# mLSTM output gate and spatial u projection with channels as rows, and the spatial mix with swapped operands

## The chip, the cores and the metric

The kernel runs as one program on one core of a Trainium2 chip. Times are device microseconds (us) of that core, from several executions of the same program; one more execution is recorded by the hardware profiler and gives the trace. Engines are named as in the trace: PE (TensorE, matrix products) with PEld (its weight loads), DVE (VectorE), ACT (ScalarE), POOL (GpSimd) and SP (SyncE, which here issues nearly all DMAs).

## The reference, cut to what matters

Two layers act on 512 latent tokens (x) and, in layer 0 only, on 256 context tokens as well (in layer 1 the context is still read, but has no output). Each layer makes one wide projection of the normalised input (1024 columns in), feeds four mixers, gates each of their outputs, projects and sums. Two of the mixers matter here:

```
# B: spatial gating, chunks of 128 tokens, 4 groups of 128 channels
u = gelu(u)
v = layer_norm(gelu(v), ln_g, ln_b)
mixed = einsum('gts,bnsgc->bntgc', w_s, v in chunks) + b_s.T[:, :, None]
yg = u * mixed

# D: mLSTM, 4 heads of 128 channels
hn = rms_norm(h_forward + h_backward, m_norm per head)
ym = sigmoid(m_o) * hn
```

u, v and m_o are 512 columns each of the wide projection. Everything is float32.

## The kernel before, in words

**Projections.** A product of two float32 matrices is made of three PE products of rounded float32 parts (high by high, high by low, low by high), so a tile of output over the 1024 inputs (8 blocks of 128) costs 24 matmuls. There are two ways to write it. `tok_mm` (line 411) keeps a block of 128 tokens stationary and streams 256 columns of weights: the result has tokens as rows. `x_seg` and `seg_mm` (lines 440 and 424) keep 128 columns of weights stationary and stream the tokens, 512 of x (`SEGX`) or 256 of context (`SEGC`): the result has channels as rows. Weights come in units of 256 columns; `take` and `emit_load` load a unit ahead in two halves, which ACT (line 224) and DVE (line 225) split into parts.

**The parts that change.** `mo_unit` (line 573) projects m_o with tokens as rows: per unit and per token tile 24 matmuls of 256 columns, a tanh on ACT (line 581), a product with the norm's weights on DVE (line 582), and a DMA to DRAM in 512-byte rows (line 583). There are 2 units of 6 token tiles in layer 0 and 2 of 4 in layer 1. `mlstm_scan` reads these rows back per head (line 1019), multiplies them into the normalised state with one DVE instruction per chunk (line 1060), turns each chunk with a PE transpose (line 1066), copies the result out of PSUM with ACT (line 1067) and writes it to `ydram[3]`.

`spatial` (line 619) projects v with tokens as rows, normalises it (`spatial_norm`), and mixes the tokens of a chunk with `spatial_mix` (line 692): four plain float32 products with the mixing weights stationary and v streamed, and four ACT instructions of 128 columns that add the bias, one number per row (line 699). Then it projects u with tokens as rows (line 654), applies gelu (`gelu2`, line 610, on tiles of 256 columns: lines 613 to 617), multiplies by the mixed v (line 662), and `turn_out` (line 673) turns the product with two PE transposes (line 676), halves it on ACT out of PSUM (line 678) and writes it to `ydram[2]` (line 679). That is 20 tiles in all, 12 in layer 0 and 8 in layer 1. `turn_out` lags two tiles behind, in the list `tails`.

**Buffers.** Tiles come from pools of fixed numbers of buffers: `T1` (256 columns, 7 buffers), `ST` (512 columns, 3 buffers, shared by the gate, early and m units, the rotary stage and the norm), `M` (768 columns, 8 buffers), `BIG` (4 buffers), and in PSUM `DB` (3 banks) for projections.

**Order.** The program is written as two interleaved threads: the mixers (attention, then the mLSTM scans) and the dense units in the order of `FILL_ORDER` (line 71), in proportion to costs given by hand (`TOK_US`, `seg_us`, `RATIO`). The mixers' instructions get a higher priority, and the tile framework then draws up the order of each engine's instructions from an estimated timeline (`schedule_with_timeline_sim=True`, line 1557). In layer 1 the spatial units run among the dense units, beside the window attention. In layer 0 they run inside `merge` (line 1266), at the places that `AFTER` (line 70) gives: branches are merged in the order 0, 1, 3, 2 with 8 steps j each, v after steps 6 and 7 of the first, `g_u0` after step 0 and `g_u1` after step 3 of the third. The last two tails are run after steps 4 and 5 (line 1343). The fourth branch is the spatial one: it reads `ydram[2]` back (line 1279) with its gate (line 1280), multiplies (line 1287) and splits into parts (lines 1288 and 1289).

Of the kernel before, what the change touches and what calls it, by code (L numbers as in the profile page):

```python
# [19 lines left out]
XT = 4  # L20
NT = 6
# [62 lines left out]
def tile_hybrid_block(ctx, tc, A, out):  # L84
# [61 lines left out]
    # constants  # L146
# [131 lines left out]
    def side(units):  # L278
        """Units of later uses, their rows of weights summed up by VectorE, in small steps."""
# [144 lines left out]
    def seg_mm(wh, wl, mh, ml, nk, seg):  # L424
        """One column tile over one token segment."""
# [44 lines left out]
    def rotate(ear, nh, t, g, tabs, copies):  # L470
        """Second stage: norm, rotary and the split into copies of high and low parts."""
# [30 lines left out]
    def drain(n2, n3):  # L502
        """Runs the waiting stages of earlier tiles, all but the last n2 and n3."""
# [106 lines left out]
    def gelu2(dst, ps, acc=None):  # L610
        """dst = 2 gelu(ps), and its sum over the columns"""
        e, sq = T1(), T1()
# [6 lines left out]
    def spatial(l, ydram, nq, tails, res):  # L619
# [18 lines left out]
        vsum = const.tile([128, NT, 2], F32, tag="vsum", name="vsum")  # L638
        for i in range(2):
            w = in_unit(l, f"g_v{i}")  # L640
            for t in range(nq):
                ps = tok_mm(w, 256, t)
                idle_drain()
                gelu2(V[:, t, i * 256:(i + 1) * 256], ps[:, :256], vsum[:, t, i:i + 1])
                if i == 1:
                    spatial_norm(V[:, t, :], vsum[:, t, :], lng, lnb)
                    if t >= 2:
                        spatial_mix(V[:, t - 2, :], sgw, sgb)
                yield TOK_US + (0.9 if i else 0.0)
            yield  # L650
        for i in range(2):
            w = in_unit(l, f"g_u{i}")
            for t in range(nq):
                ps = tok_mm(w, 256, t)
                if i == 0 and t < 2:
                    spatial_mix(V[:, nq - 2 + t, :], sgw, sgb)
                if len(tails) > 1:
                    tails.pop(0)()
                gu = T1()
                gelu2(gu, ps[:, :256])  # L660
                v = V[:, t, i * 256:(i + 1) * 256]
                dve.tensor_mul(v, v, gu)
                dst = ydram[2, 2 * i:2 * i + 2, :, t * 128:(t + 1) * 128]
                tails.append(lambda v=v, dst=dst: turn_out(v, dst))
                yield TOK_US + 0.22
            if i == 1 and res is not None:
                while tails:
                    tails.pop(0)()
# [4 lines left out]
    def turn_out(v, dst):  # L673
        pt = DB()
        for g in range(2):
# [885 lines left out]
```

## Time and profile before

| | us |
|---|---|
| three executions | 2069.32, 2072.67, 2073.26 |
| their median | 2072.67 |
| span of the profiled execution | 2072.0 |
| PE busy in it | 2006.9 |
| DVE busy | 1321.5 |
| ACT busy | 978.5 |

The span runs from the first to the last instruction of the profiled execution. A busy time is the union of an engine's instructions. A matmul's record is longer than the distance to the next one, since they are pipelined: what a matmul costs is read from the distance between starts. Layer 0 lasts to about 1235 us: the first 60 us are the prologue, then come the interleaved threads to about 860, the merge to about 1160 and the output projection. Layer 1 repeats this, without a prologue.

### The profile page before, as it was taken

What the parts mean: (1) busy time and instruction counts of PE and PEld (TensorE: products, weight loads), DVE (VectorE), ACT (ScalarE), POOL (GpSimd) and SP (SyncE); (2) the same over time, 40 slices, a digit from 0 to 9 for tenths busy, and PEclk for the clock granted to TensorE, in tenths of its full rate; (3) what the DMA queues carried; (4) which work ended last, traced back from release to release, by engine and by line L of the source; (5) the groups of instructions that cost most, each with busy time, mean ns of one, the idle gap of its engine ahead of it and who ended that gap; (6) DMA issues with size and microseconds to landing.
All of it is one profiled execution on the core that took longest, in us unless ns stands there. A gap on an engine that the chain in (4) does not pass through costs nothing. (4 is left out here: it accounts for less than half of the span.)

```text
span 2072.0 us, 34558 instructions
## 1 busy us (share of the span) xinstructions
PE 2006.9 (97%) x13196; PEld 1816.9 (88%) x13196; DVE 1321.5 (64%) x2861; ACT 978.5 (47%) x2195; POOL 69.0 (3%) x76
## 2 busy tenths in 40 slices
PE   7999999999999999999999999999999999999998
PEld 4998998999999898889998999989989898887777
DVE  5766766676556665648545588667676575555765
ACT  6565554344444444324432376655554465433333
POOL 0200100000000000001000022000000000000000
PEclk9999999999999999999999999999999999999999
DMA  7212223323333534665334352223334325447745
GB/s 279 73 44 85 81 86 115 123 98 112 122 117 96 172 122 149 198 206 184 114 116 140 123 190 67 86 96 112 92 121 139 123 90 161 147 147 224 246 136 178
DMA packets 133142, 274.97 MB, mean 133 GB/s; under 512 B 16176, under 2 KB 52208, under 8 KB 132592
## 3 DMA queue, kind: packets, MB, share of 16 engines
q1 hardware_dynamic: 132688, 272.69, 40.5%
q8 instruction: 104, 1.70, 0.3%
q14 instruction: 62, 0.51, 0.1%
q10 hardware_dynamic: 288, 0.07, 0.0%
HBM read 219.33 MB, written 53.37 MB: 132 GB/s over the span
## 5 line engine op out<-in xcount | busy, mean ns | idle before, releaser
L238 PE MATMUL d<-xh,wh 128*128 128x512 f32 (+1 forms) x1504 | 538.0, 358 | 0.1
L238 PE MATMUL d<-xh,wl 128*128 128x512 f32 (+1 forms) x1504 | 535.9, 356 | 0.0
L238 PE MATMUL d<-xl,wh 128*128 128x512 f32 (+1 forms) x1504 | 535.2, 356 | 0.0
L225 DVE TENSOR_TENSOR wl<-wr,wh 128x1024 fp32r<-128x1024 f32 (+3 forms) x274 | 294.5, 1096 | 67.9 <-ACT wh L224 64.8
L224 ACT CAST wh<-wr 128x1024 fp32r<-128x1024 f32 (+3 forms) x274 | 248.8, 950 | 182.5 <-PE s L238 81.7
L238 PEld LDWEIGHTS d<-xh,wh 128*128 128x128 f32 x1504 | 285.6, 190 | 35.0 <-DVE st L604 0.3
L238 PEld LDWEIGHTS d<-xh,wl 128*128 128x128 f32 x1504 | 285.4, 190 | 34.4
L238 PEld LDWEIGHTS d<-xl,wh 128*128 128x128 f32 x1504 | 285.6, 190 | 33.7
L238 PE MATMUL d<-wh,xh 128*128 128x256 f32 (+1 forms) x992 | 287.1, 290 | 5.6 <-ACT t L614 1.4
L238 PE MATMUL d<-wl,xh 128*128 128x256 f32 (+1 forms) x992 | 283.3, 286 | 0.3 <-DVE wl L225 0.3
L238 PE MATMUL d<-wh,xl 128*128 128x256 f32 (+1 forms) x992 | 282.5, 286 | 0.6 <-DVE xl L401 0.4
L238 PEld LDWEIGHTS d<-wh,xh 128*128 128x128 f32 x992 | 189.8, 192 | 7.2 <-ACT t L614 1.6
L238 PE MATMUL s<-big,wh 128*128 128x512 f32 x720 | 184.1, 362 | 9.6 <-DVE big L1289 8.0
L238 PEld LDWEIGHTS d<-wh,xl 128*128 128x128 f32 x992 | 190.0, 192 | 1.3 <-DVE xl L401 0.8
L238 PEld LDWEIGHTS d<-wl,xh 128*128 128x128 f32 x992 | 190.3, 192 | 0.9 <-DVE wl L225 0.5
L780 DVE TENSOR_TENSOR m<-s,m 128x768 fp32r<-128x768 f32 (+2 forms) x144 | 119.4, 836 | 95.2 <-ACT m L779 94.6
L744 ACT ACTIVATE m<-s,yx 128x768 f32<-128x768 f32 (+3 forms) x160 | 120.2, 752 | 92.8 <-DVE yx L742 46.0
L238 PEld LDWEIGHTS s<-big,wh 128*128 128x128 f32 x720 | 120.4, 191 | 32.8 <-DVE big L1289 9.2
L738 DVE TENSOR_REDUCE yx<-s 128x1 f32<-128x768 f32 (+3 forms) x160 | 122.5, 765 | 34.9 <-PE s L238 33.8
L779 ACT CAST m<-s 128x768 fp32r<-128x768 f32 (+2 forms) x144 | 100.8, 704 | 88.6 <-PE s L776 88.0
L238 PE MATMUL b<-m,v 128*128 128x256 f32 (+1 forms) x768 | 132.3, 286 | 4.0 <-ACT m L779 4.0
L238 PE MATMUL s<-big 128*128 128x256 f32 (+2 forms) x680 | 119.7, 304 | 1.3 <-ACT big L496 0.7
(289 smaller groups left out, 3035.0 us busy)
## 6 DMA issues: line engine op xcount, KB each, us to landing
wr<-in_w_in_dram SPq DMA_DIRECT2D x100, 512.0 KB, 4.2
wr<-in_w_mg_dram SPq DMA_DIRECT2D x50, 512.0 KB, 4.3
wr<-in_w_mod_dram SPq DMA_DIRECT2D x42, 512.0 KB, 5.3
wr<-in_w_out_dram SPq DMA_DIRECT2D x32, 512.0 KB, 3.7
th<-st SPq DMA_DIRECT2D x50, 256.0 KB, 4.7
wr<-in_w_bp_dram SPq DMA_DIRECT2D x50, 256.0 KB, 3.9
wr<-in_w_br_dram SPq DMA_DIRECT2D x28, 384.0 KB, 4.2
m<-th SPq DMA_DIRECT2D x26, 384.0 KB, 6.0
```

What stands on the lines that cost most here:

```text
L224: act.copy(wh[:, sl], raw[:, :hn])
L225: dve.tensor_sub(wl[:, sl], raw[:, :hn], rd(wh[:, sl]))
L238: pe.matmul(o, l, r, start=start, stop=stop)
L738: dve.reduce_max(out=mx, in_=ps[:, :n], axis=AX.X)
L744: act.activation(P, ps[:, :n], AF.Exp, bias=nm[:, 0:1], scale=sc, accum_out=sm)
L779: act.copy(ph, pt[:, :n])
L780: dve.tensor_sub(pl, pt[:, :n], rd(ph))
```

## The change

`mo_unit` and the u part of `spatial` use `x_seg`: channels as rows, weights stationary, tokens streamed in 512 or 256 columns. The norm's weights become one number per row, loaded once per layer by a DMA of single elements. The mLSTM output is normalised, transposed and then multiplied by its gate straight out of PSUM. `spatial_mix` swaps its operands (v stationary, mixing weights streamed), so its result has channels as rows like u; its bias now lies along the columns, so `bias_rows` makes a tile with the halved bias spread over rows (four DVE instructions, one float32 product, one ACT copy, once per layer), and one DVE instruction of 512 columns halves and adds. `turn_out`, `tails` and the transposes of line 676 are gone. In layer 0, where `V` has no tile to spare, the bias tile is a buffer of the `M` pool. The new tiles of `mo_unit` and of the u part (two per segment) come from `ST` in place of `T1`. The diff also drops comments and docstrings, and so moves line numbers; that part is left out here.

```diff
-    def mo_unit(l, i, omd, nq):
+    def mo_unit(l, i, omd, segs):
         w = in_unit(l, f"m_o{i}")
-        g = T1()
-        sy.dma_start(out=g, in_=bc(A["m_norm"][l, :, i * 256:i * 256 + 256], [128, 256]))
-        for t in range(nq):
-            ps = tok_mm(w, 256, t)
-            idle_drain()
-            th = T1()
-            act.activation(th, ps[:, :256], AF.Tanh, scale=0.5)
-            dve.scalar_tensor_tensor(out=th, in0=th, scalar=1.0, in1=g, op0=ALU.add, op1=ALU.mult)
-            sy.dma_start(out=omd[2 * i:2 * i + 2, :, t * 128:(t + 1) * 128].rearrange("h p d -> p h d"), in_=v3(th, 2))
-            yield TOK_US
+        if i == 0:
+            g = const.tile([128, 4], F32, tag="mnorm", name="mnorm")
+            sy.dma_start(out=g, in_=A["m_norm"][l].rearrange("o (h e) -> e (o h)", h=4))
+            res_g[l] = g
+        g = res_g[l]
+        for c in range(2):
+            h = 2 * i + c
+            for seg in segs:
+                ps = x_seg(w, c, seg)
+                idle_drain()
+                n = seg.stop - seg.start
+                th = ST()[:, :n]
+                act.activation(th, ps, AF.Tanh, scale=0.5)
+                dve.tensor_scalar(th, th, 1.0, g[:, h:h + 1], op0=ALU.add, op1=ALU.mult)
+                sy.dma_start(out=omd[h][:, seg], in_=th)
+                yield seg_us(seg)
...
+        sgr = V[:, nq, :] if nq < NT else M(512)
...
                 if i == 1:
                     spatial_norm(V[:, t, :], vsum[:, t, :], lng, lnb)
+                    if t == 1:
+                        bias_rows(sgb, sgr)
                     if t >= 2:
-                        spatial_mix(V[:, t - 2, :], sgw, sgb)
+                        spatial_mix(V[:, t - 2, :], sgw, sgr)
...
             w = in_unit(l, f"g_u{i}")
-            for t in range(nq):
-                ps = tok_mm(w, 256, t)
-                if i == 0 and t < 2:
-                    spatial_mix(V[:, nq - 2 + t, :], sgw, sgb)
-                if len(tails) > 1:
-                    tails.pop(0)()
-                gu = T1()
-                gelu2(gu, ps[:, :256])
-                v = V[:, t, i * 256:(i + 1) * 256]
-                dve.tensor_mul(v, v, gu)
-                dst = ydram[2, 2 * i:2 * i + 2, :, t * 128:(t + 1) * 128]
-                tails.append(lambda v=v, dst=dst: turn_out(v, dst))
-                yield TOK_US + 0.22
+            for c in range(2):
+                g = 2 * i + c
+                for seg in segs:
+                    ps = x_seg(w, c, seg)
+                    if g == 0 and seg.start == 0:
+                        for t in range(nq - 2, nq):
+                            spatial_mix(V[:, t, :], sgw, sgr)
+                    n = seg.stop - seg.start
+                    e = ST()[:, :n]
+                    gelu2(e, ps, e, ST()[:, :n])
+                    m = V[:, seg.start // 128:seg.stop // 128, g * 128:(g + 1) * 128]
+                    dve.tensor_mul(v3(e, n // 128), v3(e, n // 128), m)
+                    sy.dma_start(out=ydram[2, g][:, seg], in_=e)
+                    yield seg_us(seg) + 0.22
...
-    def turn_out(v, dst):
-        pt = DB()
-        for g in range(2):
-            pe.transpose(pt[:, g * 128:(g + 1) * 128], v[:, g * 128:(g + 1) * 128], ident)
-        ys = T1()
-        act.mul(ys, pt[:, :256], 0.5)
-        sy.dma_start(out=dst.rearrange("g p t -> p g t"), in_=v3(ys, 2))
+    def bias_rows(sgb, rows):
+        d = ST()
+        for g in range(4):
+            dve.tensor_scalar(d[:, g * 128:(g + 1) * 128], ident, sgb[:, g:g + 1], 0.5, op0=ALU.mult, op1=ALU.mult)
+        ps = DB()
+        mm(ps, ones, d, True, True)
+        act.copy(rows, ps)
...
-            mm(ps[:, gs], sgw[g], v[:, gs], True, True)
-        for g in range(4):
-            gs = slice(g * 128, (g + 1) * 128)
-            act.activation(v[:, gs], ps[:, gs], AF.Identity, bias=sgb[:, g:g + 1])
+            mm(ps[:, gs], v[:, gs], sgw[g], True, True)
+        dve.scalar_tensor_tensor(out=v, in0=ps, scalar=0.5, in1=sgr, op0=ALU.mult, op1=ALU.add)
...
-            dve.scalar_tensor_tensor(out=H[:, cs], in0=H[:, cs], scalar=r[:, c:c + 1], in1=om[:, cs],
-                                     op0=ALU.mult, op1=ALU.mult)
+            dve.tensor_scalar(H[:, cs], H[:, cs], r[:, c:c + 1], None, op0=ALU.mult)
...
-        act.copy(H[:, :n], pt[:, :n])
-        sy.dma_start(out=ydram[3, h][:, :n], in_=H[:, :n])
+        dve.tensor_mul(om[:, :n], pt[:, :n], om[:, :n])
+        sy.dma_start(out=ydram[3, h][:, :n], in_=om[:, :n])
...
-                    done = SPOTS[l][bi, j] == "g_u1"
-                elif done and tails:
-                    tails.pop(0)()
```

## Rows read from the trace of the kernel before

**Rows 1.** The page: busy time and share of the span, and instructions, by engine.

```profile
PE 2006.9 (97%) x13196; PEld 1816.9 (88%) x13196; DVE 1321.5 (64%) x2861; ACT 978.5 (47%) x2195; POOL 69.0 (3%) x76
```

**Rows 2.** Busy us by stretch; columns PE, PEld, DVE, ACT, POOL, PEclk, DMA, GB/s.

```profile
120.00:860.00 740.00, 731.93 (x4926) 671.68 (x4925) 474.05 (x1114) 347.89 (x805) 11.64 (x9) 0.99 0.35 114
...
1240.00:1900.00 660.00, 648.74 (x4172) 584.11 (x4173) 432.17 (x980) 348.35 (x768) 20.11 (x19) 1.00 0.37 119
```

**Rows 3.** Waits of PE: us in total, times, longest.

```profile
PE s L238 <- DVE big L1289: 8.0, 3, 2.8
...
PE b L238 <- ACT m L779: 4.0, 2, 3.0
...
PE d L495 <- ACT st L488: 3.2, 2, 1.6
```

**Rows 4.** PE in order of time, in the first u unit of layer 0.

```profile
1006.96 0.28 PE L238 MATMUL d<-wl,xh 128*128 128x256 f32 x1
...
1009.60 0.29 PE L238 MATMUL d<-wh,xl 128*128 128x256 f32 x1
1009.72 0.38 PE L676 MATMUL d<-ident,big 128*128 128x128 f32 x2
```

**Rows 5.** PE in order of time, in a unit with weights stationary, layer 1.

```profile
1654.68 0.39 PE L238 MATMUL d<-xl,wh 128*128 128x512 f32 x1
...
1656.50 0.39 PE L238 MATMUL d<-xh,wh 128*128 128x512 f32 x1
```

**Rows 6.** PE in order of time, six transposes among matmuls, layer 0.

```profile
302.06 0.82 PE L776 MATMUL s<-ident,m 128*128 128x128 f32 x6
302.64 0.36 PE L238 MATMUL d<-wh,xh 128*128 128x256 f32 x1
302.84 0.28 PE L238 MATMUL d<-wl,xh 128*128 128x256 f32 x1
```

**Rows 7.** Line 676: engine, count, duration ns min/median/max, first and last start.

```profile
L676 PE MATMUL d<-ident,big x40: 270/272/276, 1009.7 to 1708.3; 128*128 128x128 f32 x40
```

**Rows 8.** PE groups by shape, all of the span: count, busy us, mean ns.

```profile
L238 PE MATMUL d<-xh,wh 128*128 128x512 f32 x960 | 381.2, 397 | 0.1
...
L238 PE MATMUL d<-big,cT 128*2 128x256 f32 x48 | 10.8, 379 | 0.0
```

**Rows 9.** An ACT group by shape: count, busy us, mean ns, idle before.

```profile
L699 ACT ACTIVATE big<-d,sgb 128x128 f32<-128x128 f32 x40 | 11.4, 373 | 1.6 <-PE d L238 1.5
```

**Rows 10.** DVE groups by shape: count, busy us, mean ns, idle before.

```profile
L1323 DVE SCALAR_TENSOR_TENSOR m<-m,s 128x768 f32<-128x768 f32 x24 | 22.8, 952 | 42.8 <-PE s L238 39.5 <-DMA m<-th 3.2
L554 DVE SCALAR_TENSOR_TENSOR st<-st,d 128x512 f32<-128x512 f32 x32 | 21.9, 683 | 16.3 <-ACT st L553 16.0
```

**Rows 11.** SP in order of time before the fourth branch of layer 0.

```profile
1085.54 0.37 SPq L679 DMA_DIRECT2D yd<-t  x1
...
1087.40 0.33 SPq L1279 DMA_DIRECT2D m<-yd  x1
```

**Rows 12.** DVE in order of time at the start of that branch.

```profile
1094.22 0.96 DVE L1287 TENSOR_TENSOR m<-m 128x768 f32<-128x768 f32 x1 [3.48 <-DMA m<-sg]
1095.10 1.82 DVE L1289 TENSOR_TENSOR big<-m,big 128x768 fp32r<-128x768 f32 x2
```

**Rows 13.** PE in order of time there.

```profile
1096.10 0.61 PE L238 MATMUL s<-big,wh 128*128 128x512 f32 x2 [2.85 <-DVE big L1289]
```

**Rows 14.** The stretch behind it, columns as in rows 2.

```profile
1097.20:1100.50 3.30, 3.30 (x12) 2.82 (x11) 3.30 (x5) 0.61 (x1) 0.00 (x0) 0.50 1.03 325
```

**Rows 15.** SP, line 576: count, ns min/median/max, first and last start.

```profile
L576 SPq DMA_DIRECT2D t<-in_m_norm_dram x4: 328/333/424, 239.2 to 1543.3; - x4
```

**Rows 16.** ACT, line 581: count, ns min/median/max, first and last start.

```profile
L581 ACT ACTIVATE t<-d x20: 371/384/392, 290.8 to 1595.0; 128x256 f32<-128x256 f32 x20
```

**Rows 17.** A wait of ACT: us in total, times, longest.

```profile
ACT st L488 <- DMA sg<-st: 7.6, 2, 4.8
```

**Rows 18.** DVE in order of time, preparing the second branch of layer 0.

```profile
907.08 0.96 DVE L1286 TENSOR_TENSOR m<-m 128x768 f32<-128x768 f32 x1 [5.88 <-DMA m<-rs]
...
938.94 0.95 DVE L1286 TENSOR_TENSOR m<-m 128x768 f32<-128x768 f32 x1
```

More of the change, by code (lines that the diff above doesn't have):

```diff
@@ L571, in early_unit @@
                 yield seg_us(seg)
-    def mo_unit(l, i, omd, nq):
+    def mo_unit(l, i, omd, segs):
         w = in_unit(l, f"m_o{i}")
-        g = T1()
-        sy.dma_start(out=g, in_=bc(A["m_norm"][l, :, i * 256:i * 256 + 256], [128, 256]))
-        for t in range(nq):
-            ps = tok_mm(w, 256, t)
-            idle_drain()
-            th = T1()
-            act.activation(th, ps[:, :256], AF.Tanh, scale=0.5)
-            dve.scalar_tensor_tensor(out=th, in0=th, scalar=1.0, in1=g, op0=ALU.add, op1=ALU.mult)
-            sy.dma_start(out=omd[2 * i:2 * i + 2, :, t * 128:(t + 1) * 128].rearrange("h p d -> p h d"), in_=v3(th, 2))
-            yield TOK_US
+        if i == 0:
[14 more added lines that the diff above has]
+                yield seg_us(seg)
+    res_g = {}
     def m_unit(l, i, zd, res):
@@ L608, in m_unit, with gelu2 @@
                 res["done"].add(("M", h))
-    def gelu2(dst, ps, acc=None):
-        e, sq = T1(), T1()
+    def gelu2(dst, ps, e, sq, acc=None):
         act.copy(e, ps)
@@ L617, in gelu2, with spatial @@
         dve.scalar_tensor_tensor(out=dst, in0=sq, scalar=1.0, in1=e, op0=ALU.add, op1=ALU.mult, accum_out=acc)
-    def spatial(l, ydram, nq, tails, res):
+    def spatial(l, ydram, segs, res):
+        nq = segs[-1].stop // 128
         if res is not None:
@@ L643, in spatial @@
                 idle_drain()
-                gelu2(V[:, t, i * 256:(i + 1) * 256], ps[:, :256], vsum[:, t, i:i + 1])
+                gelu2(V[:, t, i * 256:(i + 1) * 256], ps[:, :256], T1(), T1(), vsum[:, t, i:i + 1])
                 if i == 1:
                     spatial_norm(V[:, t, :], vsum[:, t, :], lng, lnb)
+                    if t == 1:
+                        bias_rows(sgb, sgr)
                     if t >= 2:
-                        spatial_mix(V[:, t - 2, :], sgw, sgb)
+                        spatial_mix(V[:, t - 2, :], sgw, sgr)
                 yield TOK_US + (0.9 if i else 0.0)
@@ L652, in spatial @@
             w = in_unit(l, f"g_u{i}")
-            for t in range(nq):
-                ps = tok_mm(w, 256, t)
-                if i == 0 and t < 2:
-                    spatial_mix(V[:, nq - 2 + t, :], sgw, sgb)
-                if len(tails) > 1:
-                    tails.pop(0)()
-                gu = T1()
-                gelu2(gu, ps[:, :256])
-                v = V[:, t, i * 256:(i + 1) * 256]
-                dve.tensor_mul(v, v, gu)
-                dst = ydram[2, 2 * i:2 * i + 2, :, t * 128:(t + 1) * 128]
-                tails.append(lambda v=v, dst=dst: turn_out(v, dst))
-                yield TOK_US + 0.22
+            for c in range(2):
[12 more added lines that the diff above has]
+                    yield seg_us(seg) + 0.22
             if i == 1 and res is not None:
-                while tails:
-                    tails.pop(0)()
                 release(res, "big", 1)
@@ L690, in spatial_norm, with spatial_mix @@
         dve.scalar_tensor_tensor(out=v, in0=v, scalar=r[:, 0:1], in1=lnb, op0=ALU.mult, op1=ALU.add)
-    def spatial_mix(v, sgw, sgb):
+    def spatial_mix(v, sgw, sgr):
         ps = DB()
@@ L1102, in dense @@
                 if name == "g_v0":
-                    res["g"] = spatial(l, ydram, nq, [], res)
+                    res["g"] = spatial(l, ydram, segs, res)
                 for r in res["g"]:
@@ L1112, in dense @@
             elif name.startswith("m_o"):
-                yield from mo_unit(l, int(name[3]), omd, nq)
+                yield from mo_unit(l, int(name[3]), omd, segs)
                 res["done"].add(("O", int(name[3])))
@@ L1269, in merge @@
         segs = [SEGX, SEGC] if want_c else [SEGX]
-        tails = []
-        gating = spatial(l, ydram, NT if want_c else XT, tails, None)
+        gating = spatial(l, ydram, segs, None)
         zb = []
         zs = {}
-        done = False
         for bi, b in enumerate(BRANCHES):
@@ L1341, in merge @@
                         pass
-                    done = SPOTS[l][bi, j] == "g_u1"
-                elif done and tails:
-                    tails.pop(0)()
         pt = BIG([128, 4, NTOK], F32R)
```

## The prediction

> **What bounds the kernel now.** I read the page's busy times first: PE is busy 2006.9 of 2072.0 us, DVE 64%, ACT less than half [rows 1]. The table by stretch shows that this holds where the change lies: PE lacks 8.1 us of 740 in the interleaved part of layer 0 and 11.3 of 660 in that of layer 1 [rows 2]. So PE sets the pace there. What one of its instructions costs is the distance between starts, so I next read PE in order of time. In a unit with tokens as rows, 22 distances take 1009.60 - 1006.96 = 2.64 us: 0.120 us for 256 columns [rows 4]. In a unit with weights stationary, 8 distances take 1656.50 - 1654.68 = 1.82 us: 0.2275 for 512 [rows 5]. Two short ones cost 0.0125 more than a long one. The list of PE's waits shows what is left: single waits of 1 to 4 us, chiefly for DVE's and ACT's splitting of a branch or of attention weights [rows 3].
>
> **The projections.** Before, m_o and u each take 2 units of 6 tiles in layer 0 and of 4 in layer 1, 24 matmuls of 256 columns a tile: 2 x 20 x 24 = 960. After, each unit has two column tiles; layer 0 has a segment of 512 and one of 256 in each, layer 1 one of 512. That is 384 of 512 columns and 192 of 256 left over: 384 pairs become 384 single ones, 384 x 0.0125 = 4.8 us less on PE. The row shows a fixed part of some 13 ns that each matmul adds to its columns. The Trainium skill, page TensorE: Matmul & The Clock Gate, section Back-to-back issue gap, gives N/2.4 ns plus 2.5 for an isolated matmul, so its fixed part is 2.5 ns; by it the estimate for the pairs is 384 x 2.5 = 1.0 us and the whole sum below 3.8 us smaller.
>
> **The transposes.** Line 676 issues 40 [rows 7]. A single price is read from six of the same shape: from their first start to the second matmul behind them 302.84 - 302.06 = 0.78 us pass, of which one matmul of 256 is 0.12, so six cost 0.66 and one 0.11 us [rows 6]. Removed: 40 x 0.11 = 4.4 us of PE. Their ACT pass and their write go too.
>
> **The mix and its bias.** The swapped products are as many, with the same shape, so PE keeps them. Forty ACT instructions, 11.4 us busy [rows 9], become 10 on DVE of 512 columns from PSUM, 0.68 each [rows 10]: 6.8 us, beside PE. New on PE: one float32 product of 512 columns per layer. No row has that shape. A float32 product shows as two instructions (48 for 24 products), and one of 256 columns lasts 379 ns, nearly the 397 of a rounded one of 512 [rows 8]; so a float32 column counts double, and the product costs 2 x 2 x 0.2275 = 0.9 us. Bounds: 0.45 if it counted single, 0.9 if double; I take 0.9, twice: 1.8 us.
>
> **ACT and DVE elsewhere.** The gelu and tanh passes do the same columns in fewer instructions. Per head the gate's product moves to DVE, out of PSUM, at most 0.95 us [rows 10], for an ACT copy that goes: 8 x 0.95 = 7.6. DVE gains some 10 us in all and ACT loses over 20. Both have a third or more of their time free [rows 1], so I cost this at nothing; without that cover it is DVE's 10 us.
>
> **DMAs.** m_o and the u part issue 12 writes each in place of 20, in 1 to 2 KB rows, so SP has 16 fewer. The norm's weights come as 512 elements of 4 bytes, once a layer. No row has such a DMA. Before, its issue came 50 us ahead of the first tanh (239.2 against 290.8) [rows 15, 16]; the new one needs nothing earlier either, so it is hidden and costs 0; without the lead it could hold DVE for some us, twice.
>
> **The start of the fourth branch in layer 0.** This is the one stall that the change touches. SP issues in order. The last tail's write stands at 1085.54, and the third block's loads come only behind it, at 1087.40 [rows 11]. DVE waits 3.48 us for the third block's gate before it goes on to the split that PE waits for [rows 12]; PE stands 2.85 us [rows 13], and the 3.3 us after that run at a granted clock of 0.50, the lower level of 1.2 GHz [rows 14], which costs another 1.65. After the change the write is issued with `g_u1`, two steps earlier, and SP is free. The loads can move up by 2 to 3 us; they still need buffers. Bounds: nothing, or 2.85 + 1.65 = 4.5. I take 2.0, nearer the middle; late next is the block's own buffer.
>
> **ST.** The u part takes two of the three `ST` buffers per segment. ACT already waits for this ring, 7.6 us in two places [rows 17], and PE stood 3.2 us behind such a pair [rows 3]. A segment's own chain is three ACT passes of about 0.6 (DVE's 0.68 bounds them) and three DVE passes of 0.68, some 4 us [rows 10], and PE works 24 x 0.2275 = 5.5 us on the next. So I cost it at 0, with one such pair per layer, 6.4 us, as the other end.
>
> **Sum.** -4.8 - 4.4 + 1.8 - 2.0 = -9.4 us. Against the profiled span of 2072.0 that is 2062.6; the median of the runs is 0.7 above that span, so **2063**. A measurement of this kernel tells about 0.2%, 4.1 us, from no change.
>
> **Rivals.**
> *The saved time turns into waits.* The framework draws up every engine's order anew, and the waits of 1 to 4 us [rows 3] are where its estimate missed; three or four new ones give back 8 us: 2071, within 0.2%. For it: the sum is only half a per cent, and the stalls lie elsewhere. Against it: PE is short of work in 1 to 2% of these stretches only [rows 2], so a gap elsewhere has other work to fill it.
> *A buffer of M too few (slower).* In layer 0 the bias tile holds one of eight `M` buffers, two more are held by the spatial weights; the second and the third branch are prepared with five in place of six. The preparation is paced by these buffers: the first gate product at 907.08 waits 5.88 us for its DMA, and the fourth comes at 938.94 [rows 18], 32 us. Drawn out by 6/5 it takes 6.4 us more; with a clock dip of 1.65, 8 us a branch, 16 for two: 2072.7 - 7.4 + 16 = 2081. It decides once the preparation ends after PE has used up the v or u unit beside it. Against it: a unit of v gives PE 6 x 24 x 0.120 = 17 us of cover, and the tile may only be taken when it is written, late in that stretch.
> *The fixed part is not the matmul's own.* If the 13 ns come from the neighbours in these stretches and the pairs give 1.0 us, the sum is -5.6: 2067. Both rows come from unbroken runs of the same instruction, which speaks against it. The page named above gives this case.
> *More than the sum.* The lighter ACT and SP queues also take away two or three other stalls of 2 to 3 us with their clock dips: 2055.
>
> **How the numbers follow.** Forecast 0.58 (2057 to 2068), small fixed part 0.04, more than the sum 0.10: faster 0.72. Saved time turned into waits 0.17: same. A buffer too few, or the ST ring's 6.4 us with a wait on top, 0.11: slower. The range leaves out under 2 in 10: from 2055, the better case, to 2077, four short of the full price of the missing buffer. It takes in the bounds of the branch stall (2060 to 2065) and of ST (2070).
>
> **What would show it.** Right: PE busy falls by about 7 us with 424 matmul instructions fewer and 4 more for the bias; starts 0.2275 apart in the m_o and u units; no transposes between u tiles; the wait of PE for line 1289's successor at the fourth branch under 1 us, without the dip. Wrong: new waits of PE in layer 0's merge for the split of the second or third branch (the M buffer), ACT waiting for a DMA out of `ST` beside the u units, or DVE waiting for the norm's weights. The forecast fails if PE's busy time falls and its idle time grows by as much.

## The result, and the profile after

The changed kernel takes 2088.41 us, median of four executions (2085.31 to 2091.33), against 2070.99 for the kernel before on the same chip: a ratio of 1.0096, interval 1.0077 to 1.0116. It is slower by about 17 us, where 2063 was forecast, and lies above the range.

The page of the changed kernel, busy times by engine, answers to [rows 1]; the table by stretch below it to [rows 2], with one stretch more, the merge of layer 0. Its row in the kernel before stands last.

```profile
PE 2008.5 (96%) x12776; PEld 1797.8 (86%) x12776; DVE 1329.5 (64%) x2855; ACT 955.7 (46%) x2097; POOL 71.4 (3%) x76
```

```profile
120.00:860.00 740.00, 730.03 (x4831) 665.77 (x4830) 469.93 (x1104) 345.14 (x797) 11.65 (x9) 0.99 0.35 112
860.00:1160.00 300.00, 276.58 (x1632) 243.14 (x1631) 168.61 (x279) 88.75 (x175) 7.53 (x7) 0.96 0.48 151
1240.00:1900.00 660.00, 645.77 (x3990) 574.77 (x3990) 438.71 (x999) 344.05 (x746) 28.36 (x26) 0.99 0.36 118
```

```profile
860.00:1160.00 300.00, 288.33 (x1872) 261.74 (x1871) 171.49 (x287) 104.28 (x234) 7.53 (x7) 0.98 0.49 158
```

PE has 420 instructions fewer, as worked out (424 less 4), and yet is as busy as before; busy time also counts work at the lower clock, and the mean granted clock of the profiled execution is 0.985 against 0.988. In the merge of layer 0 PE stands 23 of 300 us at a mean granted clock of 0.96, against 12 us and 0.98 before. In the other two rows it misses 10 of 740 and 14 of 660 us, 2 and 3 more than before.

The new instructions themselves cost what was forecast. PE in order of time, in the second u unit of layer 0:

```profile
1063.69 0.39 PE L238 MATMUL d<-xl,wh 128*128 128x512 f32 x1
...
1064.60 0.39 PE L238 MATMUL d<-xh,wl 128*128 128x512 f32 x1
1064.82 0.28 PE L238 MATMUL d<-xh,wh 128*128 128x256 f32 x1
...
1066.26 0.28 PE L238 MATMUL d<-xh,wh 128*128 128x256 f32 x1
```

Four long distances take 0.91 us, 0.2275 each, twelve short ones 1.44, 0.120 each, as in [rows 4, 5].

What is new stands between 905 and 985 us, in the v unit of layer 0. First the DMA queue of SP, then DVE, then PE, in order of time:

```profile
904.96 5.62 SPq L222 DMA_DIRECT2D wr<-in_w_in_dram  x2
911.39 25.90 SPq L222 DMA_DIRECT2D wr<-in_w_bp_dram  x5
945.28 0.33 SPq L644 DMA_DIRECT2D sgb<-in_sg_b_dram  x1
945.66 0.43 SPq L1286 DMA_DIRECT2D m<-yd  x1
```

```profile
944.39 0.86 DVE L687 TENSOR_SCALAR st<-ident,sgb 128x128 f32<-128x128 f32 x4
953.77 0.95 DVE L1293 TENSOR_TENSOR m<-m 128x768 f32<-128x768 f32 x1
...
971.25 0.96 DVE L1293 TENSOR_TENSOR m<-m 128x768 f32<-128x768 f32 x1 [1.72 <-DMA m<-rs]
```

```profile
945.40 2.04 PE L238 MATMUL d<-st,ones 128*128 128x512 f32 x2 [5.79 <-ACT st L698]
962.69 0.96 PE L238 MATMUL s<-big,wh 128*128 128x512 f32 x4 [0.99 <-ACT big L1295]
...
976.26 1.65 PE L238 MATMUL s<-big,wh 128*128 128x512 f32 x4 [2.17 <-ACT big L1295]
```

The first load of the second branch (line 1286) is issued at 945.66. Ahead of it in SP's order stand five weight loads (line 222), at one of which SP waits 21.2 us for DVE's split of earlier weights, and the `sgb` load of layer 1, which waits until the bias rows have read layer 0's `sgb` (line 687). So the first gate product comes at 953.77, where [rows 18] had it at 907.08 and the fourth at 938.94. PE waits 5.79 us at the bias product and then again for the second branch's split. The stretch behind each pause runs at a granted clock of 0.50, the lower level of 1.2 GHz; columns as in [rows 2]:

```profile
944.40:951.20 6.80, 5.80 (x21) 4.79 (x22) 2.42 (x9) 1.40 (x3) 0.93 (x1) 0.50 0.61 190
975.20:982.00 6.80, 5.05 (x13) 3.68 (x14) 5.80 (x14) 2.73 (x5) 2.31 (x2) 0.50 0.58 190
```

### The profile page after: what moved, and what is told of

Same layout as the page of the kernel before. It is cut to its first block, busy times and chain, and to the rows that moved or that the text cites. A ratio compares the mean times of both kernels' runs of the same rounds, so it can differ in the third digit from the quotient of the medians.

```text
span 2089.5 us, 33552 instructions
## 1 busy us (share of the span) xinstructions
PE 2008.5 (96%) x12776; PEld 1797.8 (86%) x12776; DVE 1329.5 (64%) x2855; ACT 955.7 (46%) x2097; POOL 71.4 (3%) x76
## 5 line engine op out<-in xcount | busy, mean ns | idle before, releaser
L238 PE MATMUL d<-xh,wh 128*128 128x512 f32 (+1 forms) x1696 | 607.0, 358 | 0.2
L238 PE MATMUL d<-xh,wl 128*128 128x512 f32 (+1 forms) x1696 | 604.2, 356 | 0.0
L238 PE MATMUL d<-xl,wh 128*128 128x512 f32 (+1 forms) x1696 | 603.5, 356 | 0.0
L238 PEld LDWEIGHTS d<-xl,wh 128*128 128x128 f32 x1696 | 321.8, 190 | 38.2
L238 PE MATMUL d<-wh,xh 128*128 128x256 f32 (+1 forms) x672 | 197.8, 296 | 4.8 <-DVE xh L1443 1.9
L238 PE MATMUL d<-wh,xl 128*128 128x256 f32 (+1 forms) x672 | 193.3, 289 | 0.4 <-DVE xl L401 0.4
L238 PE MATMUL d<-wl,xh 128*128 128x256 f32 (+1 forms) x672 | 193.5, 289 | 0.0
L238 PEld LDWEIGHTS d<-wh,xh 128*128 128x128 f32 x672 | 130.7, 195 | 6.7 <-issue 2.9
L238 PEld LDWEIGHTS d<-wl,xh 128*128 128x128 f32 x672 | 131.2, 195 | 0.8 <-issue 0.8
L238 PEld LDWEIGHTS d<-wh,xl 128*128 128x128 f32 x672 | 130.4, 195 | 1.0 <-DVE xl L401 0.8
```

What stands on the lines that cost most here:

```text
L238: pe.matmul(o, l, r, start=start, stop=stop)
```

## The experiments

Three theories stood at first, all for that stretch: (1) a buffer of `M` too few, (2) the `sgb` load that blocks SP, (3) the bias product that stands in PE's order before its operands are there. For each kernel two places are read from its trace: when the output stage of layer 0 begins on DVE (the first line after the merge, 16 instructions of one shape), and how long it is from its last start in layer 0 to its first in layer 1. The rows of the kernel before and after, to show how:

```profile
L1384 DVE TENSOR_TENSOR big<-d,m x16: 415/420/425, 1157.7 to 1221.6; 128x256 f32<-128x256 f32 x16
L1384 DVE TENSOR_TENSOR big<-d,m x16: 414/418/425, 2023.7 to 2065.3; 128x256 f32<-128x256 f32 x16
```

```profile
L1388 DVE TENSOR_TENSOR big<-d,m x16: 416/422/426, 1172.8 to 1236.8; 128x256 f32<-128x256 f32 x16
L1388 DVE TENSOR_TENSOR big<-d,m x16: 414/419/426, 2041.7 to 2082.7; 128x256 f32<-128x256 f32 x16
```

That is 1157.7 and 2023.7 - 1221.6 = 802.1 before, 1172.8 and 804.9 after: by these two traces 15 us are lost in layer 0, 3 in layer 1. All runs, each ratio against the kernel before on the same chip:

| run | median us | ratio [interval] | output stage of layer 0 | layer 1 |
|---|---|---|---|---|
| before, second profile | 2067.82 | 1.0016 [1.0002, 1.0029] | 1150.4 | 802.6 |
| a_rows_own | 2082.93 | 1.0063 [1.0041, 1.0084] | 1158.3 | 813.3 |
| a_sgb_both | 2086.89 | 1.0086 [1.0065, 1.0107] | 1170.8 | 804.4 |
| b_hold_m | 2074.73 | 1.0023 [1.0004, 1.0042] | 1149.9 | 812.4 |
| a_touch | 2083.01 | 1.0078 [1.0060, 1.0096] | 1161.3 | 810.9 |
| a_early | 2079.50 | 1.0068 [1.0044, 1.0092] | 1157.1 | 808.1 |
| b_mo_only | 2077.81 | 1.0051 [1.0032, 1.0071] | 1158.0 | 804.5 |
| b_mo_256 | 2079.45 | 1.0058 [1.0039, 1.0078] | 1153.3 | 811.6 |
| b_mo_yield | 2078.04 | 1.0056 [1.0037, 1.0075] | 1154.1 | 810.0 |
| b_mo_H | 2078.87 | 1.0074 [1.0057, 1.0091] | 1160.6 | 802.0 |
| b_end_dve | 2077.78 | 1.0065 [1.0050, 1.0080] | 1149.2 | 812.4 |
| b_end_act | 2068.75 | 1.0003 [0.9989, 1.0018] | 1155.0 | 804.2 |
| b_sp_early | 2063.87 | 0.9996 [0.9981, 1.0011] | 1144.7 | 804.1 |
| b_ratio1 | 2080.63 | 1.0064 [1.0040, 1.0088] | 1150.8 | 813.7 |
| b_ratio2 | 2066.48 | 0.9999 [0.9983, 1.0015] | 1147.4 | 804.0 |
| a_ratio1 | 2095.18 | 1.0132 [1.0110, 1.0154] | 1163.9 | 815.3 |
| b_sp_ratio | 2061.55 | 0.9970 [0.9958, 0.9982] | 1143.2 | 804.1 |
| a_ratio3 | 2071.96 | 1.0015 [0.9998, 1.0033] | 1154.4 | 807.6 |

The first row is the same program as the kernel it is compared with.

> The kernel before, once more, to see in a second profile how far the stages of one kernel differ from execution to execution: the times of the runs so far go from 2061 to 2073. If these are half-clock stretches of TensorE, the second profile has fewer of them in proportion (about 0.5 us of time per us at half clock) and the same start-to-start times elsewhere.

The clock goes as expected (0.991 against 0.988), but the two trials of one program already differ by 3 us: a ratio within 0.0016 of another tells nothing. The two profiles of it differ by 7 us in layer 0 (1157.7 and 1150.4) and by 0.5 in layer 1, so a single time of layer 0 tells nothing below some 7 us.

### The loads of the second branch

`a_rows_own`, the bias rows in their own tile, with two `T1` buffers fewer to make room for it:

```diff
-        return tp.tile([128, 256], F32, tag="t1", name="t1", bufs=7)
+        return tp.tile([128, 256], F32, tag="t1", name="t1", bufs=5)
-        sgr = V[:, nq, :] if nq < NT else M(512)
+        sgr = V[:, nq, :] if nq < NT else const.tile([128, 512], F32, tag="sgr", name="sgr")
```

> The changed kernel with the bias rows of layer 0 in a tile of their own instead of a buffer of M; two of the seven t1 buffers pay for its space. Theory 1 (a buffer of M too few delays the preparation of the second branch): most of the excess goes, 2070 to 2077 us, and the loads of the second branch are issued from about 900 us on, as in the kernel before. Theory 2 (the load of layer 1's sgb, which waits for the last read of layer 0's, stands ahead of these loads in SP's order): no change unless the order of the loads changes as well; by itself 2088. Theory 3 (the bias product stands in TensorE's order before its operands are there): the product is still in the same place, 2085 to 2090, with a wait of 4 us or more at it. Fewer t1 buffers could add 0 to 4 us in every theory.

`a_sgb_both`, no `sgb` load that waits:

```diff
-        sgb = const.tile([128, 4], F32, tag="sgb", name="sgb")
-        sy.dma_start(out=sgb, in_=A["sg_b"][l])
+        if "sgb" not in both:
+            both["sgb"] = const.tile([128, 8], F32, tag="sgb", name="sgb")
+            for ll in range(2):
+                sy.dma_start(out=both["sgb"][:, 4 * ll:4 * ll + 4], in_=A["sg_b"][ll])
+        sgb = both["sgb"][:, 4 * l:4 * l + 4]
```

> The changed kernel with one sgb tile for both layers, loaded at the start, so that nothing on SP waits for the bias rows. Theory 1 (M): the loads still wait for a buffer of M, 2086 to 2090 us. Theory 2 (the sgb load blocks SP): 2071 to 2078, loads of the second branch from about 900 us on. Theory 3 (bias product in TensorE's order): 2086 to 2090.

`b_hold_m`, the kernel before with an `M` buffer held:

```diff
-        sgb = const.tile([128, 4], F32, tag="sgb", name="sgb")
+        sgb = const.tile([128, 4], F32, tag="sgb", name="sgb") if nq < NT else M(512)[:, :4]
```

> The kernel before with one change: in layer 0 sgb is loaded into a buffer of M, which it holds until the last mix, as the bias rows do in the changed kernel; layer 1 keeps its own tile, so no sgb load waits for layer 0. Theory 1 (M): slower by 8 to 16 us, 2079 to 2087. Theories 2 and 3: 2070 to 2073, no change.

Theory 2 falls: `a_sgb_both` stays at 1170.8, and PE waits 5.8 us at the product again. Without the request from `M`, layer 0 is back (1158.3). But a buffer held for as long in the kernel before costs layer 0 nothing (1149.9), so it is not the number of buffers. What the two requests differ in is their first write: a DMA at once there, the copy behind the bias product here. Hence theory 1b, tried twice. `a_touch` writes eight columns at the request; `a_early` makes the rows there:

```diff
         sgr = V[:, nq, :] if nq < NT else M(512)
+        if nq == NT:
+            dve.memset(sgr[:, :8], 0.0)
```

> The changed kernel, and the bias rows' buffer of M is written once (a memset of 8 columns) where it is requested, ahead of the v unit; it is held as long as in the changed kernel. Theory 1a (one buffer of M fewer is what costs): no change, 2086 to 2090. Theory 1b (the ring hands its buffers out in the order of the requests, and the loads of the second branch are lined up behind the first write of the bias rows' buffer, which comes only with the bias product): the loads start at about 900 us again and 12 to 15 us go, 2072 to 2077. Theory 3 (the product waits in TensorE's order): the wait at the product stays, 2085 to 2090.

```diff
         sgr = V[:, nq, :] if nq < NT else M(512)
+        bias_rows(sgb, sgr)
...
-                    if t == 1:
-                        bias_rows(sgb, sgr)
```

> The changed kernel with the bias rows made ahead of the v unit (their product right after the request of the buffer, not after the second tile of g_v1). Theory 1a: no change, 2086 to 2090. Theory 1b: as a_touch, 2072 to 2077. Theory 3: the wait of 5.8 us at the product goes or moves, and with it 6 to 10 us: 2078 to 2083, with the loads of the second branch still at about 945 us.

DVE in order of time in `a_touch`, the gate products of the second branch, as in [rows 18]:

```profile
915.38 0.96 DVE L1295 TENSOR_TENSOR m<-m 128x768 f32<-128x768 f32 x1 [2.99 <-DMA m<-rs]
...
945.67 0.96 DVE L1295 TENSOR_TENSOR m<-m 128x768 f32<-128x768 f32 x1 [2.19 <-DMA m<-rs]
```

They are back at 915 to 946, where the changed kernel had 954 to 971, with the buffer held exactly as long. Layer 0 gains 11.5 us by a memset of eight columns, and 15.7 with the rows made early. PE does not wait at the bias product in either, so the wait of 5.79 went with the rest, and theory 3 has no price of its own here. What costs, then, is the late first write of a buffer requested early: with it, the loads of the second branch, which request their buffers later, stand late in SP's order.

It is the order and not a wait for the write. In `a_sgb_both` the first load goes out 10 us before the copy that writes the bias rows even starts; what it stood behind is the weight loads. SP, then ACT, in order of time:

```profile
906.62 26.03 SPq L222 DMA_DIRECT2D wr<-in_w_bp_dram  x5
932.70 0.43 SPq L1289 DMA_DIRECT2D m<-yd  x1
```

```profile
942.71 0.58 ACT L693 COPY m<-d 128x512 f32<-128x512 f32 x1 [2.16 <-PE d L238]
```

In `a_touch` the first load is out at 900.65, ahead of these weight loads. A framework that hands out a pool's buffers in the order of the requests would draw up such an order; that reading was not tested further. As whole times the gains are smaller than in layer 0, 5.4 us in `a_touch` and 8.9 in `a_early`, since layer 1 takes 6 and 3 us longer than in the changed kernel, and the intervals of their ratios overlap with its interval. Both miss their 2072 to 2077; there is a second loss.

### The output gate's part alone

`b_mo_only` is the kernel before with `mo_unit` and the end of `mlstm_scan` as changed.

> The kernel before with only the output gate's part of the change (m_o with channels as rows, gate applied after the mLSTM transposes); the spatial part is as before. The prediction's sum gives 192 of the 384 pairs: -2.4 us, 2068.5. If the lag of the attention and mLSTM thread in layer 0 and the missing gain of layer 1 come from this part: 2071 to 2076. If the whole excess belongs to the spatial part, as theories 1 to 3 say, it is not above 2072.

It costs 10 us. Three variants of it follow. `b_mo_256`:

```diff
-            for seg in segs:
+            for seg in (slice(o, o + 256) for o in range(0, segs[-1].stop, 256)):
...
-                th = ST()[:, :n]
+                th = T1()
...
-                yield seg_us(seg)
+                yield TOK_US
```

> The output gate's part alone, but in segments of 256 columns with t1 buffers and the planner's step of the kernel before (2.65 per segment, as many steps as before): weights stationary and the gate after the transposes stay, pairs of matmuls don't join. Theory A (the gate's new place at the end of each mLSTM head costs it): 2076 to 2079 as in b_mo_only. Theory B (longer segments move the planner's steps, and dense work runs ahead of the attention thread) and theory C (the ring of three st buffers, shared with the gates, holds TensorE): 2068 to 2071, as the kernel before.

`b_mo_yield`:

```diff
-                yield seg_us(seg)
+                for _ in range(n // 256):
+                    yield TOK_US
```

> The output gate's part alone with its 512-column segments and st buffers, but reporting to the planner the number and cost of the steps of the kernel before (one step of 2.65 per 256 columns). Theory A: 2076 to 2079. Theory B: 2066 to 2070. Theory C: 2076 to 2079.

`b_mo_H`:

```diff
-        dve.tensor_mul(om[:, :n], pt[:, :n], om[:, :n])
-        sy.dma_start(out=ydram[3, h][:, :n], in_=om[:, :n])
+        dve.tensor_mul(H[:, :n], pt[:, :n], om[:, :n])
+        sy.dma_start(out=ydram[3, h][:, :n], in_=H[:, :n])
```

> The output gate's part alone, but each head's gated rows go into H's own buffer and are stored from there, so the gate's buffer of M is free after the multiplication and not after the store. Theory A1 (that buffer of M, held through the store, delays what follows on the ring): 2066 to 2071. Theory A2 (VectorE in ScalarE's place at the end of a head), theory D (the unit m_o itself): 2076 to 2079.

All stay at 2078 to 2079.5, so the `M` buffer held through the store (A1), the planner's steps (B) and the `ST` ring (C) fall as single causes. But they seem to lose in different places: `b_mo_H` and `b_mo_only` in layer 0 (1160.6, 1158.0, against 1150.4 in the second profile of before, though 1157.7 in its first), `b_mo_256` in layer 1 (811.6). Two edits of the kernel before at the end of each head, `b_end_dve` and `b_end_act` (no gate moved):

```diff
-        act.copy(H[:, :n], pt[:, :n])
-        sy.dma_start(out=ydram[3, h][:, :n], in_=H[:, :n])
+        dve.tensor_copy(om[:, :n], pt[:, :n])
+        sy.dma_start(out=ydram[3, h][:, :n], in_=om[:, :n])
```

```diff
-        act.copy(H[:, :n], pt[:, :n])
-        sy.dma_start(out=ydram[3, h][:, :n], in_=H[:, :n])
+        act.copy(om[:, :n], pt[:, :n])
+        sy.dma_start(out=ydram[3, h][:, :n], in_=om[:, :n])
```

> The kernel before with one change at the end of each mLSTM head: the transposed rows are copied out of PSUM by VectorE into the gate's buffer of M and stored from there, where ScalarE copied them into H; the gate and its unit stay as they were. Theories A1 and A2: 2076 to 2079. Theory D: 2065 to 2070, as the kernel before.

> The kernel before, where the end of each mLSTM head is copied by ScalarE as before, but into the gate's buffer of M and stored from there. Theory A2 (VectorE in ScalarE's place costs): 2063 to 2069, as the kernel before. Theory R (each edit that moves the order in which the scheduler lines up the instructions costs 5 to 13 us, since the order before is a favourable one): 2070 to 2078, as b_end_dve.

VectorE in place of ScalarE (A2) seemed to be it, but DVE's copies take under 1 us each, eight in all, and all of the loss sits in layer 1 (812.4). `b_hold_m`, whose edit is in layer 0 alone, shows the same 812.4. No run moves the copy from one engine to the other with the order held, so what the engine itself costs has no price here. Instead the order was moved by itself, with no operation changed, in `b_ratio1` and in `b_ratio2`:

```diff
-RATIO = ((1.5, 1.3, 1.5), (1.2, 0.4, 1.5))
+RATIO = ((1.48, 1.3, 1.5), (1.2, 0.4, 1.5))
```

```diff
-RATIO = ((1.5, 1.3, 1.5), (1.2, 0.4, 1.5))
+RATIO = ((1.5, 1.3, 1.5), (1.18, 0.4, 1.5))
```

> The kernel before with one constant of the planner changed by 1.3%: the share of dense work per unit of attention in layer 0's first phase is 1.48 in place of 1.5. All operations, operands, buffers and engines are the same, only their order moves, from layer 0's attention on. Theory A2 and every theory that puts the loss down to an operation of the change: 2062 to 2069. Theory R: 2070 to 2078.

> As b_ratio1, but in layer 1's first phase, 1.18 in place of 1.2: the order moves in layer 1 alone. Theories of an operation: 2062 to 2069. Theory R: 2070 to 2078, with the loss behind the last mLSTM head of layer 1 (about 1880 us on) and half-clock stretches there.

`b_ratio1` loses 11.6 us by 1.3% of a planner's constant, all of it in layer 1; `b_ratio2`, which moves the order too, loses nothing. So a moved order can cost as much as the whole output gate's part, but need not. Where it does, PE shows it: what a head lacks is cover, other matmuls in PE's order while the head's norm and gate run on ACT and DVE. PE in order of time at the last head of layer 1, from the last product with the head's state (`s<-xs,big`) to its transposes, first in `b_ratio2`, then in `b_ratio1`:

```profile
1875.20 0.39 PE L238 MATMUL s<-xs,big 128*128 128x129 f32 x2
...
1883.38 0.76 PE L1066 MATMUL s<-ident,m 128*128 128x128 f32 x3 [0.23 <-DVE m L1060]
```

```profile
1883.68 0.38 PE L238 MATMUL s<-xs,big 128*128 128x129 f32 x2
...
1886.84 1.23 PE L238 MATMUL d<-big,wh 128*128 128x512 f32 x3 [1.61 <-ACT big L1288]
...
1892.92 0.30 PE L1066 MATMUL s<-ident,m 128*128 128x128 f32 x1 [4.16 <-DVE m L1060]
```

From that product to the transposes 8 to 9 us pass in both, for the head's norm and gate on ACT and DVE. In the first PE has 7.5 us of other matmuls lined up in that time (counted in the trace, 0.2275 us each), in the second 2.5, and it stands. The 60 us about that head, in `b_ratio2` and in `b_ratio1` (columns as in [rows 2]), have the same clock, but PE stands 4.0 and 9.1 us:

```profile
1860.00:1920.00 60.00, 55.97 (x249) 45.09 (x248) 36.29 (x68) 19.86 (x42) 1.01 (x1) 0.97 0.68 209
```

```profile
1860.00:1920.00 60.00, 50.89 (x239) 40.78 (x238) 30.86 (x64) 17.11 (x39) 1.01 (x1) 0.97 0.62 196
```

The same wait at the same transposes is 4.20 us in `b_hold_m`, 3.16 in `b_end_dve`, 2.95 in `b_mo_256`, with 812 to 814 in the table. `b_mo_yield`, `a_touch` and `a_rows_own` lose 7 to 11 us of layer 1 without a wait at that place. Between 1800 and 1960 us their longest waits of PE are others, 3.9 and 4.4 for ACT's split of a branch in the first two, two of 3.2 for DVE in the third, and no run tests these; that part of the loss stays open. Clock dips add to it in some: in `b_end_dve` the 60 us have a mean clock of 0.89, in the kernel before 1.00 (its second profile).

```profile
1860.00:1920.00 60.00, 52.25 (x222) 41.99 (x221) 33.73 (x68) 15.80 (x37) 1.01 (x1) 0.89 0.64 202
```

```profile
1860.00:1920.00 60.00, 55.38 (x255) 44.73 (x255) 34.86 (x67) 19.40 (x42) 1.01 (x1) 1.00 0.68 213
```

In layer 0 the same cover goes in another way. Two lines, with the last write of the early units' th (the end of the dense thread) and the end of attention, in the second profile of before and in `b_mo_only`:

```profile
L570 SPq DMA_DIRECT2D th<-st x52: 319/326/1208, 337.6 to 863.4; - x52
L794 DVE TENSOR_TENSOR xs<-b,xs x48: 402/417/419, 118.8 to 725.9; 64x256 f32<-64x256 f32 x48
```

```profile
L570 SPq DMA_DIRECT2D th<-st x52: 319/320/625, 336.5 to 852.4; - x52
L802 DVE TENSOR_TENSOR xs<-b,xs x48: 402/417/419, 118.0 to 742.7; 64x256 f32<-64x256 f32 x48
```

Dense work ends 11 us earlier and attention 17 us later: PE does the same work in another order, and the third and fourth mLSTM heads are left with little beside them: between the third head's last product with its state and its transposes stand 1.5 us of other matmuls, 9.1 before (counted in the two traces). PE in `b_mo_only`, where the last side products are followed by two bare waits for the state, 1.90 and 0.79 us:

```profile
850.48 1.84 PE L238 MATMUL d<-ones,t 128*128 128x1 f32 x16
854.22 1.22 PE L238 MATMUL b<-m 128*128 128x129 f32 x4 [1.90 <-ACT xs L1036]
856.24 1.23 PE L238 MATMUL b<-m 128*128 128x129 f32 x4 [0.79 <-DVE xs L1038]
```

### The spatial part alone, and the cover put back

`b_sp_early` is the kernel before with the spatial part as changed and the rows made early as in `a_early`.

> The kernel before with the spatial part of the change alone (u with channels as rows, the mix with swapped operands, no transposes, bias rows), its bias rows made ahead of the v unit; the output gate is as before. If the whole of the spatial part's excess was the late first write of the bias rows' buffer, its share of the sum is left: 192 pairs x 0.0125 = -2.4, 40 transposes -4.4, bias product +1.8, stall of the fourth branch -2.0, so -7 us: 2059 to 2063 against 2066 to 2068 for the kernel before on such chips. If something else in it costs as well: 2066 to 2074.

Its ratio is 0.9996, no difference that shows: of the 7 us that the sum gives this part 0.8 came as time, by the interval at most 3.9. Its PE busy time, 1999.6 us, is 3.7 below the second profile of before; that of `b_sp_ratio` below, the same operations, is 6.1 below it. Two profiles of the kernel before differ by 3.6 in the same number. `a_ratio1` tried to bring the attention threads forward with lower shares of dense work (`RATIO` 1.46, 1.27, 1.5 and 1.12, 0.37, 1.5):

> The changed kernel with early bias rows and the planner's shares of dense work lowered by 2 to 7% (1.46, 1.27, 1.5 in layer 0, 1.12, 0.37, 1.5 in layer 1), so that the attention threads, which end 14 and 31 us later than before, get ahead again. If the late thread costs the rest of the excess: 2060 to 2070. Theory A2: 2076 to 2082. Theory R: anywhere from 2062 to 2080, with no relation to the lag.

It is the slowest of all; the lag grew (the last start of that line of attention is 761.0, in `a_early` 740.3). Lower shares were the wrong handle. The last two raise the share in the mLSTM phase alone, on the spatial part (`b_sp_ratio`) and on the whole change with early rows (`a_ratio3`):

```diff
-RATIO = ((1.5, 1.3, 1.5), (1.2, 0.4, 1.5))
+RATIO = ((1.5, 1.3, 1.7), (1.2, 0.4, 1.7))
```

> The spatial part alone with early bias rows, and the planner's share of dense work in the mLSTM phase of both layers 1.7 in place of 1.5; no operation differs from b_sp_early. In TensorE's order the dense work between the last step of a head and its transposes is then 9.5 us for the last head of layer 0 (5.4 before) and 6.4 for that of layer 1 (4.1). Theory L (what is lost beside the bias rows is cover of the last mLSTM heads: dense work that stands elsewhere in the order): 2056 to 2062, below both kernels. Theory R without a place (any order costs by luck): 2058 to 2078.

> The changed kernel with early bias rows and the same share, 1.7 in the mLSTM phase. In TensorE's order the dense work between the last step and the transposes of layer 0's third head is 6.1 us (1.6 without the new share, 8.9 in the kernel before), for the fourth head it stays at 3.4; layer 1 has 0.2 and 7.5 for its last two. Theory L: 2070 to 2077, below 2079.5, still above the kernel before. Theory A2 (VectorE at the end of a head): 2077 to 2082.

Both fall into the ranges of theory L, lost cover; 2061.55 lies in that of theory R, any order by luck, as well. The stretch of layer 0's last heads and the start of the merge, in `b_mo_only`, in the second profile of before, in `b_sp_early` and in `b_sp_ratio`:

```profile
850.00:950.00 100.00, 87.95 (x554) 78.35 (x553) 60.76 (x134) 32.95 (x93) 4.57 (x4) 0.91 0.68 211
```

```profile
850.00:950.00 100.00, 91.12 (x609) 82.86 (x608) 59.43 (x125) 35.01 (x90) 3.92 (x4) 0.97 0.67 210
```

```profile
850.00:950.00 100.00, 91.20 (x627) 83.58 (x626) 61.62 (x135) 34.42 (x86) 4.24 (x4) 0.98 0.62 199
```

```profile
850.00:950.00 100.00, 95.51 (x648) 86.22 (x646) 62.06 (x134) 34.58 (x89) 4.24 (x4) 1.00 0.65 205
```

PE stands 12, 9, 9 and 4.5 us of the 100, and the clock goes with it. The last two differ in the share alone. For the whole change the same comparison, `a_early` and then `a_ratio3`, does not show it:

```profile
850.00:950.00 100.00, 88.31 (x562) 78.91 (x561) 59.66 (x136) 33.30 (x94) 3.64 (x3) 0.90 0.65 200
```

```profile
850.00:950.00 100.00, 88.40 (x583) 79.77 (x582) 59.63 (x135) 33.95 (x94) 4.26 (x4) 0.93 0.66 204
```

PE stands 12 us in both, and the stage times are 2.7 and 0.5 us apart, within what two profiles of one program differ by. The two bare waits for the state are gone from the stretch, but a wait of 3.4 for DVE (line 694) has come. The profiled execution of `a_ratio3` took 2076.49, 4.5 above its median; where the 0.0053 of the ratio between the two runs is saved, its trace does not tell.

`b_sp_ratio` beats both kernels: 0.9970, 0.9958 to 0.9982. Its page against that of before's second profile:

```profile
PE 1997.2 (97%) x12968; PEld 1798.5 (87%) x12968; DVE 1326.4 (64%) x2855; ACT 961.2 (47%) x2113; POOL 71.8 (3%) x76
```

```profile
PE 2003.3 (97%) x13196; PEld 1813.4 (88%) x13196; DVE 1321.8 (64%) x2861; ACT 978.5 (47%) x2195; POOL 68.8 (3%) x76
```

The new share was not tried on the kernel before by itself. So how much of the 0.3% it would bring without the spatial part is open, and so is how much of the gain of `a_ratio3` is the change's lost cover put back and how much any kernel of this kind would gain.

## Why the prediction was wrong

- **Pairs, transposes:** right. Starts are 0.2275 and 0.120 apart in the changed units, the 40 transposes are gone, and the spatial part's PE busy time fell by 3.7 and 6.1 us in two runs where its terms say 2.4 + 4.4 - 1.8 = 5.0. The rival with the smaller fixed part falls: the rows show some 13 ns after the change as before. The Trainium skill (page TensorE: Matmul & The Clock Gate, section Back-to-back issue gap) gives 2.5 ns for an isolated matmul; these streams do not agree with that figure.
- **Bias product:** forecast 0.9 each; in layer 1 its row lasts 1.13 us (a duration, longer than the distance to the next start). In layer 0 it took 2.04 at half clock, behind a wait of 5.79 that no step had: the product's place in PE's order was not costed.
- **DMAs, ST:** right. The norm's weights are issued at 28.7 and 662.4 and nothing waits for them; PE's waits behind an `ST` pair sum to 3.9 us against 3.2 [rows 3].
- **Fourth branch:** 2.0 forecast, and about 1.9 came, by another way. PE still waits 2.57 us there (2.85 in [rows 13]), since DVE now waits 2.79 for the fourth block's gate: the third's first load is out at 1095.18, 17 us ahead, and the fourth's only at 1104.52 and 1105.39, behind the third's gate load, at which SP waits 4.2 us. That fits "late next is the block's own buffer" but does not show it. What went is the half clock behind the wait, which no term had going by itself, so that the sizes agree is luck.
- **A buffer of M too few** had the place and nearly the size (16 us, and 2081), at a chance of 0.11, and the wrong reason, so that its nearness is luck: holding one costs layer 0 nothing (`b_hold_m`). The sentence that I set against it, that the tile may be taken only when it is written, late in that stretch, is the failure: with a late write the loads of the branch stand behind five weight loads in SP's order (first load at 945.66), and with an early one ahead of them (900.65 in `a_touch`), for 11.5 to 15.7 us of layer 0.
- **The saved time turns into waits** was right in kind and too small: 8 us for the whole, where the output gate's part alone takes back its 2.4 and 10 more. The failing step is the one set against it, that a gap has other work to fill it. PE is short in 1 to 2% of a stretch because the order leaves work beside each mLSTM head. A change that moves the order can take it away at the last heads: in `b_ratio1` 2.5 us of other matmuls are left there and PE stands 4.16, in `b_ratio2` 7.5 and it stands 0.23.
- **DVE and ACT at nothing:** right as durations; `b_end_dve` shows 13 us from moving a copy of under 1 us, and `b_ratio1` 11 from moving none.

Together: in layer 0 some 12 to 16 us for the late first write, of which 5 to 9 came back as whole time, and the rest (10 and the 2.4 not saved, in the output gate's part by itself) most likely for cover lost beside the last mLSTM heads. That the late first write costs its part is shown by three kernels without it (`a_rows_own`, `a_touch`, `a_early`) and one that holds the buffer without it (`b_hold_m`). That order alone can cost as much as the second part is shown by `b_ratio1`, and that a larger share brings some 11 us of the whole change back, by the ratios of `a_early` and `a_ratio3`; that lost cover is the whole of the second part is argued, not shown. Which edit of the output gate moves the order so is not settled: in 512-column segments it seems to be layer 0 that loses, in 256-column segments layer 1.

## What to carry to other kernels

Request a pool's buffer where it is first written, or write it where it is requested: here a request with a late first write put the loads that request theirs after it late in the queue's order. Where a scheduler lines up the instructions, judge a change of half a per cent only after moving the order on purpose, once without any change of work; here that alone was worth 11 us. Look for the loss at the end of a latency chain, and count the matmuls that stand in PE's order beside it.

## What was not expected of the hardware

One program's executions spread with the clock: the kernel before took 2061.90 at a mean granted clock of 0.992 and 2072.63 at 0.988 on one chip. Pauses of PE of 5.79 and 2.17 us were followed by stretches at 0.50, at 944.4 and 975.2 above. In the first of them PE is busy 5.80 us at half rate, so that some 2.9 us of work are lost on top of the pause. But not always: behind the 2.57 us at the fourth branch of the changed kernel it stayed at 1.00:

```profile
1112.70:1116.00 3.30, 3.24 (x18) 2.82 (x19) 3.30 (x6) 0.00 (x1) 0.00 (x0) 1.00 0.71 238
```
